# A hybrid encoder layer on one core: the split operands of each FFN phase moved to another byte offset in their buffers

## The chip, the core and the metric

The kernel runs on one core of a Trainium2 chip. The metric is the device time of one execution in microseconds, and lower is better. The program computes a whole encoder layer in float32 for 1024 rows of 1024 numbers.

## The reference, cut to what matters

```python
def swiglu_half_step(x, gain, w_in, w_out):          # w_in: 1024 x 5632, w_out: 2816 x 1024
    h = rms_norm(x, gain)
    gate, up = jnp.split(h @ w_in, 2, axis=-1)
    return (jax.nn.silu(gate) * up) @ w_out

x = x + 0.5 * swiglu_half_step(x, ffn1_norm, ffn1_w_in, ffn1_w_out)
x = x + hybrid_mixer(x, ...)      # attention heads and HGRN2 heads side by side, two projections
x = x + 0.5 * swiglu_half_step(x, ffn2_norm, ffn2_w_in, ffn2_w_out)
x = rms_norm(x, final_norm)
```

## The kernel before, in words

**Order of the work.** The program has four parts that follow each other: the first FFN (0 to about 750 us), the mixer's input projections with the recurrent heads (to about 1170 us), the attention with the output projections (to about 1410 us), and the second FFN. Each FFN has an up phase (`ffn_up`) and a down phase (`ffn_down`). A scheduler of the framework decides in which order each engine's instructions stand; within a pool, a tile waits until its buffer is free.

**Split operands.** Every large product is made of matmuls in the type float32r on TensorE. To keep float32 accuracy each operand is split into a high part and a low part (`split`, L98 to L103): ScalarE casts the source into the first half of a tile `hl` of shape [128, 2, 512] (L102), and VectorE writes source minus high part into the second half (L103). A product of two split operands is three matmuls: high by high, high by low, low by high. In a matmul one operand is stationary (loaded into the array by a weight load, PEld in the profile), and the other moves through it. In a row of the profile `py_ffn<-hl_out_ffn,hl_act_ffn` the result stands first, then the moving operand, then the stationary one.

**Up phase.** For 20 of the 22 blocks of 128 hidden units the up phase uses a Strassen-like scheme (`unit`, L293): seven products of 12 matmuls each, 84 matmuls of 128x128 by 128x512 per block, 1680 per FFN. The stationary operand is a split weight block, tile `hl_in_...` of the pool `wop`; the moving operand is a split activation block, tile `ffn_B` or `ffn_T` of the pools B and T, which lie at the high end of SBUF (`side="right"`) and stay for the whole phase. The first two blocks use plain products (`plain`, L276): 384 matmuls per FFN, 256 columns wide. Raw weights come by DMA into the pool `raw`, two tiles of 512 KB per block; the row tiles of x at the start of the phase use the same pool.

**Down phase.** For two groups g of four row tiles, and for the 22 blocks f, `operands` loads and splits the activations (`hl_act`, pool `ah`) and two halves of the weights (`hl_out_<ffn>_<f>_<g>_<d>`, pool `wo`), and `step` (L401) does 24 matmuls of 512 columns: 1056 per FFN. Here the stationary operand is `hl_act` and the moving one is `hl_out`. The last two blocks of a group (`tail`) are held back and done tile by tile.

**Where the buffers lie.** The start of a buffer in its partition, in the built program, as the remainder of its byte address by 64. Within a tile the matmuls' operands start at multiples of 512 bytes, so this remainder holds for every matmul.

| product | moving, before | stationary, before | moving, after | stationary, after |
|---|---|---|---|---|
| up, first FFN (L293, L276) | B, T: 32 | wop: 0 | 0 | 32 |
| up, second FFN | B, T: 32 | wop: 0 | 0 | 48 |
| down, first FFN (L401) | wo: 0 | ah: 0 | 0 | 16 |
| down, second FFN | wo: 0 | ah: 0 | 16 | 16 |
| mixer projections (L166, L494) | 32 | 32 | 0 | 0 |
| attention scores `s` (L797) | kT: 32 | qT: 0 | 0 | 0 |
| output projection `py` (L854) | hl_wor: 32 | recT: 0 | 0 | 0 |
| output projection `pa` (L854) | hl_woa: 32 | oT: 32 | 0 | 0 |
| attention values (L829) | pT: 32 | v_attn: 32 | 0 | 0 |

Before, the buffers of `wop`, `wo` and `ah` lie 4096 bytes apart; after, 4160 bytes (65 times 64).

The functions that the change touches, and what calls them:

Of the kernel before, what the change touches and what calls it, by code (L numbers as in the profile page):

```python
# [12 lines left out]
F32 = mybir.dt.float32  # L13
F32R = mybir.dt.float32r
# [7 lines left out]
P = 128  # L22
T = 1024
D = 1024
# [20 lines left out]
class Trunk:  # L45
    def __init__(self, ctx, tc, io):
        self.tc, self.nc, self.io = tc, tc.nc, io
        nc = self.nc
        pool = lambda name, **kw: ctx.enter_context(tc.tile_pool(name=name, **kw))
        self.const = pool("const", bufs=1)  # L50
        self.gpool = pool("gains", bufs=1)
        self.stat = pool("stat", bufs=4)
        self.dpool = pool("scratch", bufs=1, space=bass.MemoryType.DRAM)
        self.ident = self.const.tile([P, P], F32, name="ident")
        make_identity(nc, self.ident)
        self.banks = {}

# [111 lines left out]
                )  # L169


    def bank(self, name):
        return self.ps(name, "u")

# [12 lines left out]
    def ffn_up(self, name, pair, act, early_lo, mid):  # L187
# [53 lines left out]
            return [raw[j][:, k * 512 : (k + 1) * 512] for j in range(2) for k in range(2)]  # L241

        def weight_op(f, key, src, lo_engine=None):
            hl = self.wop.tile([P, 2, 512], F32R, name=f"hl_in_{name}_{f}_{key}", tag="wop")
            self.split(hl, src, lo_engine)
            return hl

# [51 lines left out]
        def unit(f):  # L299
# [8 lines left out]
            nc.scalar.copy(p1, a)  # L308
            yield
            b = bank("pb")  # L310
            product(b, A["A12"], "B21", True)
            g0 = result("g0", f)
# [34 lines left out]
        for f in range(early):  # L347
            A[f] = [weight_op(f, f"A{i}", src, early_lo) for i, src in enumerate(raw_weights(f))]
            plain(f, 0, A[f])
# [21 lines left out]
    def ffn_down(self, name, act, load, done, finish=None):  # L371

        nc = self.nc
        w_out = self.io[f"{name}_w_out"]
        tail = 2

        def operands(f, g):  # L380
            raw = self.draw.tile([P, 1024], F32, name=f"raw_out_{name}_{f}_{g}", tag="raw")
            nc.sync.dma_start(raw, w_out[f * P : (f + 1) * P, :])
            ar = self.ar.tile([P, 2, 256], F32, name=f"raw_act_{name}_{f}_{g}", tag="ar")
            nc.sync.dma_start(
                ar, act[f].rearrange("p (h t) -> p h t", h=2)[:, :, g * 256 : (g + 1) * 256]
            )
            ah = self.ah.tile([P, 2, 512], F32R, name=f"hl_act_{name}_{f}_{g}", tag="ah")
            self.split(ah, ar.rearrange("p h t -> p (h t)"))
            wo = []
            for d in range(2):  # L390
                hl = self.wo.tile([P, 2, 512], F32R, name=f"hl_out_{name}_{f}_{g}_{d}", tag="wo")
                self.split(hl, raw[:, d * 512 : (d + 1) * 512])
                wo.append(hl)
            return ah, wo

        def step(f, t, ops, py):
            ah, wo = ops
            o = (t % 2) * 256 + (t % 4) // 2 * P
            for d in range(2):
                for i, (a, b) in enumerate(((0, 0), (0, 1), (1, 0))):  # L400
                    nc.tensor.matmul(  # L401
                        py[d], ah[:, a, o : o + P], wo[d][:, b, :],
                        start=(f == 0 and i == 0), stop=(f == NF - 1 and i == 2),
                    )

        for g in range(2):
            tiles = range(4 * g, 4 * g + 4)
            py = {t: [self.bank(f"py_{name}_{t}_{d}") for d in range(2)] for t in tiles}
            x = {}
            late = []  # L410
            for f in range(NF):
                ops = operands(f, g)
                if f == 2:
                    for t in tiles:
                        x[t] = load(t)
                if f < NF - tail:
                    for t in tiles:
                        step(f, t, ops, py[t])
                else:
                    late.append((f, ops))  # L420
            for t in tiles:
                for f, ops in late:
                    step(f, t, ops, py[t])
                for d in range(2):
                    ds = slice(d * 512, (d + 1) * 512)
                    nc.vector.scalar_tensor_tensor(
                        out=x[t][:, ds], in0=py[t][d], scalar=0.5, in1=x[t][:, ds],
                        op0=ALU.mult, op1=ALU.add,
                    )
                done(t, x[t])  # L430
        if finish:
            finish()
# [535 lines left out]
def open_pools(ctx, tc, prefix, side="left", **spec):  # L968
    return {
        key: ctx.enter_context(  # L970
            tc.tile_pool(name=f"{prefix}_{key}", bufs=bufs, side=side, reuse_waits="tile")
        )
        for key, bufs in spec.items()
    }


def trunk_kernel(tc, io):
    nc = tc.nc
    with ExitStack() as ctx:
        k = Trunk(ctx, tc, io)  # L980
        rows = lambda a: [a[t * P : (t + 1) * P, :] for t in range(NT)]
        d = {key: rows(k.scratch(key, (T, D))) for key in ("x1", "x2", "x3", "xn2")}
# [9 lines left out]
        def ffn(ctx, name, xn_pair, load, done, d_spec, opened, early_lo, mid=None, finish=None):  # L992
            def sbuf(c, key, bufs, **kw):
                return c.enter_context(
                    tc.tile_pool(name=f"{name}_{key}", bufs=bufs, reuse_waits="tile", **kw)
                )

            k.open_psum(ctx, name, u=(8, 512))
            with ExitStack() as up:
                k.B, k.T = sbuf(up, "B", 4, side="right"), sbuf(up, "T", 3, side="right")  # L1000
                k.raw, k.wop, k.sums, k.snap, k.cc = (
                    sbuf(up, key, n)
                    for key, n in (("raw", 7), ("wop", 9), ("s", 4), ("n", 3), ("c", 4))
                )
                k.ffn_up(name, xn_pair, act, early_lo, mid)
            with ExitStack() as down:
                k.draw, k.ar, k.wo, k.ah = (
                    sbuf(down, key, n) for key, n in (("draw", 3), ("ar", 3), ("wo", 7), ("ah", 4))
                )
                pools = open_pools(down, tc, f"{name}_d", **d_spec)  # L1010
                opened(pools)
                k.ffn_down(name, act, lambda t: load(pools, t), lambda t, x: done(pools, t, x), finish)
# [3 lines left out]
        with ExitStack() as c1:  # L1016
            gain = []

            def pair1(i):
                x = []  # L1020
                for t in (2 * i, 2 * i + 1):
                    xt = k.raw.tile([P, D], F32, name=f"x_{t}", tag="raw")
                    nc.sync.dma_start(xt, x_in[t])
                    x.append(xt)
                if not gain:
                    gain.append(k.gain_row("ffn1_norm"))
                for xt, t in zip(x, (2 * i, 2 * i + 1)):
                    junk = k.wop.tile([P, D], F32R, name=f"junk_{t}", tag="wop").bitcast(F32)
                    k.norm_rows(xt, gain[0], xt, f"n0_{t}", junk=junk)
                return x  # L1030

            def load1(pools, t):
                xt = pools["x"].tile([P, D], F32, name=f"x0_{t}", tag="x")
                nc.sync.dma_start(xt, x_in[t])
                return xt

            gain_m = []

            def opened1(pools):
                k.hpool = hstack.enter_context(  # L1040
                    tc.tile_pool(name="hm", bufs=4, side="right", reuse_waits="tile")
                )
                hm.extend(k.new_h("hm"))
                k.wpool = hstack.enter_context(
                    tc.tile_pool(name="w2", bufs=3, side="right", reuse_waits="tile")
                )
                gain_m.append(k.gain_row("mix_norm"))

            def done1(pools, t, x):
                nc.sync.dma_start(d["x1"][t], x)  # L1050
                xns[t] = pools["xn"].tile([P, D], F32, name=f"xn_n1_{t}", tag="xn")
                k.norm_rows(x, gain_m[0], xns[t], f"n1_{t}", HALVES)
                if t >= 4:
                    k.rows_to_h(xns[t - 4], hm, t - 4, "n1", "u")

            def finish1():
                for t in range(4, NT):
                    k.rows_to_h(xns[t], hm, t, "n1", "u")

            ffn(c1, "ffn1", pair1, load1, done1, dict(x=4, xn=5), opened1, nc.gpsimd, lambda: k.vectors(k.raw), finish1)  # L1060

        with ExitStack() as c2:
# [92 lines left out]
```

## Time and profile before

| | us |
|---|---|
| median of 3 runs | 2145.54 |
| lowest and highest run | 2141.98, 2145.81 |
| the profiled execution, its own time | 2140.14 |
| its span, first to last instruction | 2138.4 |

All times in the profile are microseconds of this one profiled execution; means of one instruction are nanoseconds. PE is TensorE's matmuls, PEld its weight loads, DVE is VectorE, ACT is ScalarE, POOL is GpSimd, SP issues most DMAs. Matmuls are pipelined, and a matmul's shown duration reaches into the next ones. So the pace of the matmuls (start to start) is not the mean duration; it is read from a window in which nothing else runs on PE, or from a piece of the chain of waits, as length over count. In a window, a matmul counts if any of it lies inside, so the pace is (window + one duration) / count.

### The profile page before, as it was taken

How to read it: one execution, taken by the hardware profiler on the slowest of the kernel's cores; microseconds unless marked ns; L12 is line 12 of the kernel's file. 1: busy time of each engine (PE TensorE's matmuls, PEld its weight loads, DVE VectorE, ACT ScalarE, POOL GpSimd, SP SyncE). 2: the span in 40 equal slices, each digit the busy share in tenths (PEclk: the TensorE clock that was granted, in tenths of full speed). 3: DMA queues.
4: the chain of work that ended last, by engine and by line, in shares of the span. 5: the costliest groups of instructions: out<-in, count | busy, mean ns of one | idle time of the engine just before them, and what ended most of it. 6: DMA issues, size and time to landing. Idle time of an engine off the chain costs nothing.

```text
span 2138.4 us, 27958 instructions
## 1 busy us (share of the span) xinstructions
PE 2059.3 (96%) x10849; PEld 1754.6 (82%) x10849; DVE 1156.3 (54%) x1951; ACT 780.6 (37%) x1295; POOL 391.5 (18%) x278
## 2 busy tenths in 40 slices
PE   5899999999999999999999999988999999999998
PEld 5788878887888798989999788878888888878886
DVE  6555554535363515798872567754554554443634
ACT  4333343324343323333332546623333333333432
POOL 2333232210000000121120323313322222100000
PEclk9999999999999999999999999999999999999999
DMA  5422322127464211121234522353322221264542
GB/s 166 123 80 79 93 83 80 60 70 251 147 226 142 81 36 44 40 76 34 89 98 142 177 98 80 110 191 113 90 89 76 73 89 55 74 234 142 185 148 79
DMA packets 208124, 232.12 MB, mean 109 GB/s; under 512 B 9444, under 2 KB 169464, under 8 KB 207992
## 3 DMA queue, kind: packets, MB, share of 16 engines
q1 hardware_dynamic: 205688, 221.95, 32.9%
q0 software_dynamic: 2304, 8.39, 1.0%
q8 instruction: 85, 1.39, 0.3%
q14 instruction: 47, 0.39, 0.1%
HBM read 175.78 MB, written 54.53 MB: 108 GB/s over the span
## 4 chain that ended last, share of the span: by engine, by line
PE 91%; DVE 5%; DMA 2%; ACT 1%; issue 1%; POOL 0%; SPq 0%; DVEq 0%; ACTq 0%; POOLq 0%
PE py_ffn L401 22%; PE pa_ffn L293 16%; PE pd_ffn L293 10%; PE rec_ps L166 6%; PE pb_ffn L293 5%; PE pc_ffn L293 5%; PE pp_ffn L276 4%; PE ri_ps L494 2%; PE rg_ps L494 2%; PE py L854 2%; PE lv L560 2%; PE s L797 2%; PE pa L854 2%; PE pv L829 2%; PE aq_ps L494 1%; PE av_ps L494 1%
## 5 line engine op out<-in xcount | busy, mean ns | idle before, releaser
L401 PE MATMUL py_ffn<-hl_out_ffn,hl_act_ffn 128*128 128x512 f32 x2112 | 483.6, 391 | 3.5 <-ACT hl_out_ffn L102 3.4
L401 PEld LDWEIGHTS py_ffn<-hl_out_ffn,hl_act_ffn 128*128 128x128 f32 x2112 | 398.4, 189 | 87.8 <-ACT hl_out_ffn L102 5.0
L103 DVE TENSOR_TENSOR hl_out_ffn<-raw_out_ffn,hl_out_ffn 128x512 fp32r<-128x512 f32 x176 | 120.2, 689 | 235.7 <-ACT hl_out_ffn L102 235.5
L293 PE MATMUL pa_ffn<-ffn_T,hl_in_ffn_S 128*128 128x512 f32 x960 | 243.8, 396 | 0.0
L293 PEld LDWEIGHTS pa_ffn<-ffn_T,hl_in_ffn_S 128*128 128x128 f32 x960 | 180.9, 188 | 44.3
L102 ACT CAST hl_out_ffn<-raw_out_ffn 128x512 fp32r<-128x512 f32 x176 | 107.8, 620 | 266.8 <-PE py_ffn L401 251.2
L103 DVE TENSOR_TENSOR hl_in_ffn_S<-s_ffn,hl_in_ffn_S 128x512 fp32r<-128x512 f32 x160 | 162.6, 1019 | 30.5 <-ACT hl_in_ffn_S L102 30.5
L102 ACT CAST hl_in_ffn_S<-s_ffn 128x512 fp32r<-128x512 f32 x160 | 99.1, 621 | 204.6 <-PE pd_ffn L293 177.7
L103 DVE TENSOR_TENSOR hl_in_ffn_A<-raw_in_ffn,hl_in_ffn_A 128x512 fp32r<-128x512 f32 x128 | 101.0, 794 | 127.0 <-ACT hl_in_ffn_A L102 127.0
L102 ACT CAST hl_in_ffn_A<-raw_in_ffn 128x512 fp32r<-128x512 f32 x136 | 83.8, 624 | 182.5 <-PE pc_ffn L293 78.6
L166 PE MATMUL rec_ps<-hm,hl_rec_w 128*128 128x512 f32 x576 | 134.9, 392 | 0.0
L293 PE MATMUL pd_ffn<-ffn_T,hl_in_ffn_S 128*128 128x512 f32 x480 | 125.4, 396 | 0.0
L293 PE MATMUL pb_ffn<-ffn_B,hl_in_ffn_A 128*128 128x512 f32 x480 | 125.2, 397 | 0.0
L166 PEld LDWEIGHTS rec_ps<-hm,hl_rec_w 128*128 128x128 f32 x576 | 107.1, 188 | 21.8
L293 PE MATMUL pa_ffn<-ffn_B,hl_in_ffn_A 128*128 128x512 f32 x480 | 120.1, 399 | 0.0
L293 PE MATMUL pc_ffn<-ffn_T,hl_in_ffn_A 128*128 128x512 f32 x480 | 118.9, 396 | 0.0
L293 PE MATMUL pd_ffn<-ffn_B,hl_in_ffn_S 128*128 128x512 f32 x456 | 113.1, 397 | 0.0
L293 PEld LDWEIGHTS pa_ffn<-ffn_B,hl_in_ffn_A 128*128 128x128 f32 x480 | 90.9, 190 | 21.9
L293 PEld LDWEIGHTS pd_ffn<-ffn_T,hl_in_ffn_S 128*128 128x128 f32 x480 | 90.5, 188 | 22.1
L293 PEld LDWEIGHTS pc_ffn<-ffn_T,hl_in_ffn_A 128*128 128x128 f32 x480 | 90.4, 188 | 22.1
L293 PEld LDWEIGHTS pb_ffn<-ffn_B,hl_in_ffn_A 128*128 128x128 f32 x480 | 90.4, 188 | 21.9
L276 PE MATMUL pp_ffn<-ffn_B,hl_in_ffn_A 128*128 128x256 f32 x768 | 98.6, 289 | 7.3 <-ACT ffn_B L184 3.9
(245 smaller groups left out, 3128.8 us busy)
## 6 DMA issues: line engine op xcount, KB each, us to landing
raw_in_ffn<-in_ffn_w_in SPq DMA_DIRECT2D x88, 512.0 KB, 4.1
raw_out_ffn<-in_ffn_w_out SPq DMA_DIRECT2D x88, 512.0 KB, 3.7
raw_act_ffn<-d_act SPq DMA_DIRECT2D x88, 256.0 KB, 4.0
d_act<-g_ffn SPq DMA_DIRECT2D x80, 256.0 KB, 2.1
x<-d_x SPq DMA_DIRECT2D x24, 512.0 KB, 4.4
x<-in_x SPq DMA_DIRECT2D x16, 512.0 KB, 4.7
d_x<-x SPq DMA_DIRECT2D x16, 512.0 KB, 2.8
raw_rec_w<-in_w_in_mix SPq DMA_DIRECT2D x12, 512.0 KB, 3.8
```

Of the source, the lines that this page charges most:

```text
L102: nc.scalar.copy(hl[:, 0, :], src)
L103: (lo_engine or nc.vector).tensor_sub(hl[:, 1, :], src, hl[:, 0, :].bitcast(F32))
L166: nc.tensor.matmul(out, hl[:, a, ks], h[half][b][:, k, cols], start=(k == 0 and i == 0), stop=(k == NK - 1 and i == 2),)
L276: nc.tensor.matmul(ps[j][:, odd * 256 : (odd + 1) * 256], A[2 * j + k // 4][:, a, ks], B[k // 4][:, b, k % 4, cols], start=(k == 0 and i = ...
L293: nc.tensor.matmul(ps, A[:, a, ks], T[key][:, b, k, :], start=(first and k == 0 and i == 0), stop=(k == 3 and i == 2), skip_group_check=True,)
L401: nc.tensor.matmul(py[d], ah[:, a, o : o + P], wo[d][:, b, :], start=(f == 0 and i == 0), stop=(f == NF - 1 and i == 2),)
L494: nc.tensor.matmul(ps[:, tt, :], h[half][a][:, k, ts], hl[k // 4][:, b, ws], start=(k == 0 and i == 0), stop=(k == NK - 1 and i == 2),)
L560: nc.tensor.matmul(pl[:, cs], now[:, 0, cs], now[:, 1, cs], start=True, stop=True)
L797: nc.tensor.matmul(ps[:, ks], qT[:, a, qs], kT[:, b, kv, ks], start=(i == 0), stop=(i == 2))
L829: nc.tensor.matmul(ps, vt[:, j, a, vs], pT[j][:, b, i4, :], start=(st == 0 and i == 0), stop=(st == NT - 1 and i == 2),)
L854: nc.tensor.matmul(py, lhs(a, n), units[n][:, b, ds], start=(n == 0 and i == 0), stop=(n == 3 and i == 2),)
```

## The change

A tile of 32 bytes per partition is put at the high end of SBUF ahead of all others there, which moves every high-end buffer down by 32 bytes, to a multiple of 64. The tiles of `wop`, `ah` and `wo` become 1040 numbers long instead of 1024, and the split operand starts a few numbers into its tile: 8 numbers (32 bytes) for the first FFN's weight blocks, 12 (48 bytes) for the second's, 4 (16 bytes) for the activations of both down phases, 0 and 4 for the down weights of the first and the second FFN. The pool `raw` has 6 buffers instead of 7, and `wo` 6 instead of 7. No arithmetic is changed. Lines of the changed kernel stand up to 7 further down than those of the kernel before.

```diff
         self.ident = self.const.tile([P, P], F32, name="ident")
+        pool("align", bufs=1, side="right").tile([P, 8], F32, name="align")
...
+    def offset(self, pool, name, tag, o):
+
+        return pool.tile([P, 1040], F32R, name=name, tag=tag)[:, o : o + 1024].rearrange(
+            "p (a b) -> p a b", a=2
+        )
...
-            hl = self.wop.tile([P, 2, 512], F32R, name=f"hl_in_{name}_{f}_{key}", tag="wop")
+            hl = self.offset(self.wop, f"hl_in_{name}_{f}_{key}", "wop", 8 if name == "ffn1" else 12)
...
-            ah = self.ah.tile([P, 2, 512], F32R, name=f"hl_act_{name}_{f}_{g}", tag="ah")
+            ah = self.offset(self.ah, f"hl_act_{name}_{f}_{g}", "ah", 4)
...
-                hl = self.wo.tile([P, 2, 512], F32R, name=f"hl_out_{name}_{f}_{g}_{d}", tag="wo")
+                hl = self.offset(self.wo, f"hl_out_{name}_{f}_{g}_{d}", "wo", 0 if name == "ffn1" else 4)
...
-                    for key, n in (("raw", 7), ("wop", 9), ("s", 4), ("n", 3), ("c", 4))
+                    for key, n in (("raw", 6), ("wop", 9), ("s", 4), ("n", 3), ("c", 4))
...
-                    sbuf(down, key, n) for key, n in (("draw", 3), ("ar", 3), ("wo", 7), ("ah", 4))
+                    sbuf(down, key, n) for key, n in (("draw", 3), ("ar", 3), ("wo", 6), ("ah", 4))
...
-                    junk = k.wop.tile([P, D], F32R, name=f"junk_{t}", tag="wop").bitcast(F32)
+                    junk = k.wop.tile([P, 1040], F32R, name=f"junk_{t}", tag="wop").bitcast(F32)[:, 0:D]
```

The scheduler's order changes in a few places. On SP, at the start of the program, these are the first weight loads of the up phase before (`raw_in_ffn_<f>_<half>`, `x` the row tiles, `d_t_ffn` a store of a sum of row tiles, which waits for VectorE):

```order
L236 DMA raw_in_ffn_0_0_264<-in_ffn_w_in 128x8x128
L236 DMA raw_in_ffn_0_1_266<-in_ffn_w_in 128x8x128
L236 DMA raw_in_ffn_1_0_382<-in_ffn_w_in 128x8x128
L471 DMA g_attn_q_norm<-in_attn_q_norm 128x128
L471 DMA g_attn_k_norm<-in_attn_k_norm 128x128
L471 DMA g_rec_out_norm<-in_rec_out_norm 128x128
L223 DMA d_t_ffn_137<-t_ffn_0_500 128x512
L236 DMA raw_in_ffn_1_1_384<-in_ffn_w_in 128x8x128
L1023 DMA x_533<-in_x 128x1024
```

And the same place now:

```order
L243 DMA raw_in_ffn_0_0_268<-in_ffn_w_in 128x8x128
L243 DMA raw_in_ffn_0_1_270<-in_ffn_w_in 128x8x128
L478 DMA g_attn_q_norm<-in_attn_q_norm 128x128
L478 DMA g_attn_k_norm<-in_attn_k_norm 128x128
L478 DMA g_rec_out_norm<-in_rec_out_norm 128x128
L230 DMA d_t_ffn_141<-t_ffn_0_504 128x512
L243 DMA raw_in_ffn_1_0_386<-in_ffn_w_in 128x8x128
L243 DMA raw_in_ffn_1_1_388<-in_ffn_w_in 128x8x128
L1030 DMA x_537<-in_x 128x1024
```

The first weight tile of block 1 has moved behind the store of the first sum: it has no seventh buffer to go to.

On ACT, in the first FFN's down phase, at the change from the first group of row tiles to the second, these are the casts of the second group's weights for blocks 1 and 2 (`hl_out_ffn_<f>_<g>_<d>`), between the squares of the finished rows (`xn_n`), before:

```order
L102 CAST hl_out_ffn_1_1_0_4838<-raw_out_ffn_1_1_4831 128x512
L120 ACTIVATE xn_n_0_4673,ss_n_0_4674<-x_0_3971 128x512 x2
L120 ACTIVATE xn_n_1_4705,ss_n_1_4706<-x_1_3973 128x512 x2
L120 ACTIVATE xn_n_2_4737,ss_n_2_4738<-x_2_3975 128x512
L102 CAST hl_out_ffn_1_1_1_4841<-raw_out_ffn_1_1_4831 128x512
L120 ACTIVATE xn_n_2_4737,ss_n_2_4738<-x_2_3975 128x512
```

And now:

```order
L121 ACTIVATE xn_n_0_4677,ss_n_0_4678<-x_0_3975 128x512 x2
L121 ACTIVATE xn_n_1_4709,ss_n_1_4710<-x_1_3977 128x512 x2
L121 ACTIVATE xn_n_2_4741,ss_n_2_4742<-x_2_3979 128x512
L103 CAST hl_out_ffn_1_1_0_4842<-raw_out_ffn_1_1_4835 128x512
L121 ACTIVATE xn_n_2_4741,ss_n_2_4742<-x_2_3979 128x512
L103 CAST hl_out_ffn_1_1_1_4845<-raw_out_ffn_1_1_4835 128x512
```

Block 1's first weight half is cast where its second half was cast before, and the second half one square later. On PE the matmuls of the phases stand in the same order but for some twelve of them at this place and a few in the attention.

## The prediction

> **What bounds the kernel now.** I began with the page: engines, clock and the chain of work that ended last.
>
> ```profile
> span 2138.4 us, 27958 instructions
> PE 2059.3 (96%) x10849; PEld 1754.6 (82%) x10849; DVE 1156.3 (54%) x1951; ACT 780.6 (37%) x1295; POOL 391.5 (18%) x278
> ...
> PEclk9999999999999999999999999999999999999999
> ...
> PE 91%; DVE 5%; DMA 2%; ACT 1%; issue 1%; POOL 0%; SPq 0%; DVEq 0%; ACTq 0%; POOLq 0%
> ```
>
> TensorE is the bound: 91% of the chain, at a clock that is nearly always the full one. No other engine is busy for much over half the time. So what counts is the pace of the matmuls, start to start, and the second view is the windows of PE, over stretches in which only one product runs: up phase of the first FFN, its down phase, then the same two of the second FFN.
>
> ```profile
> 120.00:490.00 370.00, 370.00 (x1580) 1.00 0.25 78
> 500.00:600.00 100.00, 100.00 (x443) 1.00 0.63 204
> ...
> 1510.00:1880.00 370.00, 370.00 (x1581) 1.00 0.24 76
> 1900.00:2000.00 100.00, 100.00 (x443) 1.00 0.58 194
> ```
>
> The columns are the window, its length, PE's busy time with the matmuls in it, the clock, and DMA. The groups by line give the duration of one matmul:
>
> ```profile
> L401 PE MATMUL py_ffn<-hl_out_ffn,hl_act_ffn 128*128 128x512 f32 x2112 | 483.6, 391 | 3.5 <-ACT hl_out_ffn L102 3.4
> L293 PE MATMUL pa_ffn<-ffn_T,hl_in_ffn_S 128*128 128x512 f32 x960 | 243.8, 396 | 0.0
> ```
>
> Up: (370 + 0.396) / 1580 = 234.4 ns per matmul. Down: (100 + 0.391) / 443 = 226.6 ns. Both are 128x128 by 128x512 in the same type at full clock, with PE never idle, and both phases give the same in both FFNs. The difference of 7.8 ns needs a cause, and the table of buffer positions offers one: in the up phase the moving operand starts 32 bytes off the stationary one (by the remainder of 64), in the down phase both start alike. Four pieces of the chain of waits, each one product at a stretch, test this. Their columns are start, length and what.
>
> ```profile
> 30.46 22.53 PE pp_ffn L276 x192
> ...
> 798.59 38.11 PE rec_ps L166 x168
> ...
> 1120.96 46.09 PE rg_ps L494 x384
> ...
> 1205.61 5.15 PE py L854 x22
> ```
>
> `rec_ps` has both operands at 32, a distance of 0, and runs at 38.11 / 168 = 226.8 ns, the pace of the down phase, whose operands are both at 0. `py` in the attention has 32 against 0 and runs at 5.15 / 22 = 234.1 ns, the pace of the up phase. So the common position does not matter here, but the distance does: 0 gives 226.6, 32 gives 234.4. For 256 columns it looks different: `rg_ps` (distance 0) 46.09 / 384 = 120.0 ns, `pp` (distance 32) 22.53 / 192 = 117.3. At distance 0 the second 256 columns cost 226.8 - 120.0 = 106.8 ns, so 512 columns alone 213.6, and 13.2 ns lie beside the columns in each matmul. 213.6 is as low as a matmul of 512 columns can come by these rows.
>
> The trace holds only the distances 0 and 32. The change puts the up phase of the second FFN at 48 and the down phase of the first at 16. These two are the unknowns.
>
> **The change part by part**, against the profiled execution (span 2138.4, own time 2140.14 us). This is 5.4 us below the median of the three runs, 2145.54, so I add the sum to the median. A measurement of this kernel can tell about 0.2%, or 4.3 us, from no change.
>
> *First FFN, up, 1680 matmuls.* Before 0 against 32, now 32 against 0: the distance by 64 stays 32, and I take nothing. The ends: if it matters which operand is ahead, they go to 226.6 (1680 x -7.8 ns = -13.1 us), or lose as much again (+13.1).
>
> *Second FFN, up, 1680 matmuls.* From distance 32 to 48. By 64 bytes, 48 is 16 away from 0 and 16 away from 32, so neither row is nearer. I take the middle, 230.5 ns: 1680 x -3.9 = -6.6 us. The ends are the two rows: 0 and -13.1 us. Beyond them, the columns alone would be 1680 x -20.8 = -34.9 us, and as far above 234.4 as 0 is below it, +13.1.
>
> *First FFN, down, 1056 matmuls.* From distance 0 to 16, again in the middle of the two: 1056 x +3.9 = +4.1 us; ends 0 and +8.2 us, beyond them 1056 x -13.0 = -13.7 (columns alone) and +16.5.
>
> *Second FFN, down, 1056 matmuls.* Both at 16, distance 0. As 32 and 32 ran like 0 and 0, I take nothing; the end is +8.2 us, if a start that is no multiple of 32 costs as much as a distance.
>
> *Attention, 384 matmuls.* `s` and `py` go from distance 32 to 0. At -7.8 ns each that is -3.0 us. Not all of it arrives, since PE waits there for ACT and DVE at times:
>
> ```profile
> 1190.00:1440.00 250.00, 232.75 (x1396) 0.97 0.39 130
> ...
> L797 PE MATMUL s<-kT,qT 128*128 128x512 f32 x192 | 54.1, 418 | 6.8 <-ACT p L804 2.5 <-DVE qT L103 2.2 <-DVE kT L103 1.6
> ```
>
> PE is busy for 232.75 of 250 us. I take -2.0 us, ends -3.0 and 0.
>
> *Everything else on PE.* Mixer projections, `pa` and the attention values keep distance 0. The 256-column products of the second FFN move between 117.3 and 120.0 at most, 384 x 2.7 ns = 1.0 us; I take nothing.
>
> *Writing at offsets.* The splits on ACT and DVE now write at 16, 32 or 48. The trace has such writes at 32 (`pT`) beside those at 0 (`hl_out`):
>
> ```profile
> L103 DVE TENSOR_TENSOR hl_out_ffn<-raw_out_ffn,hl_out_ffn 128x512 fp32r<-128x512 f32 x176 | 120.2, 689 | 235.7 <-ACT hl_out_ffn L102 235.5
> L820 DVE TENSOR_TENSOR pT<-ptp,pT 128x512 fp32r<-128x512 f32 x64 | 43.0, 686 | 5.9 <-ACT pT L819 5.5
> ```
>
> 689 and 686 ns: nothing. And DVE mostly waits for ACT, which waits for PE, so a few per cent here would stay hidden.
>
> *One raw buffer less.* A load takes 4.1 us and a block of the up phase 84 x 0.2344 = 19.7 us; six tiles still hold three blocks. What now waits longer on SP's queue are the stores behind these loads, and nothing near reads them. At the start the first weight tile of block 1 stands behind a store that issued at 13.62 us:
>
> ```profile
> raw_in_ffn<-in_ffn_w_in SPq DMA_DIRECT2D x88, 512.0 KB, 4.1
> ```
>
> ```profile
> 13.62 0.36 SPq L223 DMA_DIRECT2D d_t_ffn<-t_ffn  x1
> ...
> 16.26 0.38 SPq L236 DMA_DIRECT2D raw_in_ffn<-in_ffn_w_in  x1
> ```
>
> Two loads are then issued where one was, at about 16 us, and land some 4 to 5 us later. Block 0's 192 matmuls begin only at 30.46, by the chain above. So this costs nothing, at most 1 us.
>
> *One `wo` buffer less.* At the change of groups the held-back blocks 20 and 21 keep four buffers and block 0 of the next group two, so block 1's weights are split later. The timelines of ACT and of DVE there, and the window of PE:
>
> ```profile
> 605.08 0.62 ACT L102 CAST hl_out_ffn<-raw_out_ffn 128x512 fp32r<-128x512 f32 x1
> ...
> 613.45 0.62 ACT L102 CAST hl_out_ffn<-raw_out_ffn 128x512 fp32r<-128x512 f32 x1
> ```
>
> ```profile
> 615.42 0.69 DVE L426 SCALAR_TENSOR_TENSOR x<-py_ffn,x 128x512 f32<-128x512 f32 x1
> ```
>
> ```profile
> 606.00:626.00 20.00, 20.00 (x90) 1.00 0.80 278
> ```
>
> By the order, block 1's first half moves from the row at 605.08 to about the one at 613.45, and its second half a cast or two behind it; with VectorE's subtraction (689 ns, after some of the norm's work) both are there by about 618. The held-back work is 4 x 12 matmuls, block 0 then runs for 24, so that block 1 is wanted some 18 matmuls (4.1 us) after the last of the held-back ones. These end at about 615, since DVE takes up their last tile at 615.42; so it is wanted near 619. PE was busy for all of these 20 us. I take nothing, and at most 1.5 us in each FFN.
>
> **The sum:** 0 - 6.6 + 4.1 + 0 - 2.0 + 0 = -4.5 us, thus 2145.5 - 4.5 = 2141.0 us. This case's own range is -9 to 0.
>
> [...]
>
> **The rivals.**
>
> *Cheap distances.* 48 runs as well as 0 (-13.1) and 16 costs nothing: with the attention -15.1 us, 2130.4; better than that if the 13.2 ns beside the columns shrink. For it: distance 0 is not free either, so some other distance may be better. Against it: the only other distance in the trace is worse.
>
> *Dear distances (slower).* Any distance but 0 sets the pace of 32: the second up phase stays (0), the first down phase goes to 234.4 (+8.2), attention -2.0: +6.2 us, 2151.7. The place is the window 500 to 600 us, and it decides from 5.9 ns per matmul on, where 1056 of them outweigh the attention and 4.3 us. For it: two rows cannot tell a smooth cost from a step.
>
> *The pitch (slower).* Buffers now lie 65 x 64 bytes apart instead of 4096. If the distance counts by 128 and not by 64, it changes from buffer to buffer: half of the second down phase gets 64 against 0 (528 x 7.8 = +4.1), the first down phase 16 or 80 (+8.2), attention -2.0: +10.3 us, 2155.8, and up to 25 if some distance is worse than 32. For it: every row before has the same distance by 128 within its kind, so none excludes it.
>
> *No effect.* The up phase differs from the down phase in something other than position, such as which operand stays for the phase. Then nothing moves, 2145.5 (at most 1 us either way). Against it: `py` and `rec_ps` have little in common with the phases whose pace they share. [...]
>
> **How the numbers follow.** Chances: the forecast 0.30, cheap distances 0.24, dear distances 0.20, the pitch 0.14, no effect 0.12. Faster by over 0.2%: all of cheap distances and 0.18 of the forecast, whose middle lies just beyond 4.3 us: 0.42. Within 0.2%: the rest of the forecast 0.12, no effect 0.12, and 0.01 of dear distances: 0.25. Slower: 0.19 + 0.14 = 0.33. The range goes from 2120 (cheap distances and a third of what lies down to the columns alone) to 2160 (the pitch with 4 us more). It leaves out about 0.1 below, where both new distances come near the columns alone, and 0.06 above.
>
> **What would show it.** In the changed profile, the same windows of PE: 120 to 490 us should hold 1580 matmuls (234.4 ns), 500 to 600 some 436 (230.5), the second FFN's up phase some 1607 in 370 us (230.5), and its down phase 443 in 100 us (226.6). `py` should take 22 x 0.2267 = 4.99 us, not 5.15. Between 606 and 626 us PE should have no idle time, and its first product of 256 columns should begin near 30.5 us. It is wrong if the first up phase or the second down phase changes its pace, since for these the rows of before say nothing should; if 16 or 48 runs above 234.4 or below 226.6; or if PE waits for weights.

## The result, and the profile after

The changed kernel takes 2151.12 us (median of 10 runs, 2147.00 to 2155.85), the kernel before 2144.52 us (10 runs on the same chip, 2139.16 to 2148.66). The ratio is 1.0033, 95% interval 1.0022 to 1.0045: slower by some 6.6 us, where 4.5 us less than before was forecast.

The first two lines of the page of the changed kernel:

```profile
span 2148.7 us, 27893 instructions
...
PE 2062.9 (96%) x10849; PEld 1753.0 (82%) x10849; DVE 1162.0 (54%) x1951; ACT 780.0 (36%) x1295; POOL 391.8 (18%) x278
```

TensorE is still the bound, with 90% of the chain of waits, so the question is again the pace of the matmuls and what holds up the starts of the phases. The windows of PE in the changed kernel (stretch, length, busy time and matmuls, clock, DMA):

```profile
120.00:490.00 370.00, 370.00 (x1586) 1.00 0.26 79
500.00:600.00 100.00, 100.00 (x431) 1.00 0.60 197
606.00:626.00 20.00, 20.00 (x88) 1.00 0.67 214
1190.00:1440.00 250.00, 231.52 (x1357) 0.97 0.38 127
1510.00:1880.00 370.00, 370.00 (x1603) 1.00 0.26 79
1900.00:2000.00 100.00, 100.00 (x434) 1.00 0.61 205
```

First FFN, up phase: (370 + 0.394) / 1586 = 233.5 ns, before 234.4. Second up phase: 370.394 / 1603 = 231.1. The two down phases: 100.395 / 431 = 232.9 and 100.395 / 434 = 231.3, before 226.6 in both. So the up phases got a little faster and both down phases much slower, the second one too, for which nothing was forecast. The chain of waits of the changed kernel has the products beside the FFNs and the end of the first FFN's start:

```profile
66.81 1.09 PE pt_ffn_T L188 x4
67.90 23.31 PE pp_ffn L283 x188
...
100.65 2.95 PE pa_ffn L300 x12
...
804.86 38.11 PE rec_ps L167 x168
...
1200.99 4.63 PE py L861 x20
```

`rec_ps` keeps its pace (226.8 ns); `py` goes to 4.63 / 20 = 231.5 ns, not to 226.7. And the last plain products of the first FFN begin at 67.90. In the chain of the kernel before, the same two pieces:

```profile
65.20 23.44 PE pp_ffn L276 x188
...
97.38 3.32 PE pa_ffn L293 x12
```

They began 2.7 us earlier, and so did the up phase behind them, by 3.3 us. The starts of the phases in the two traces show where the profiled 10.3 us went (2148.7 against 2138.4; the profiled run of before was 4.4 us under its median of ten, the one of after 0.6 us, so 3.8 us of it is scatter):

| stretch | longer by, us |
|---|---|
| start to first up-phase matmul | 3.3 |
| first up phase | -1.8 |
| first down phase and its norm | 6.0 |
| mixer | 0.0 |
| attention | 1.4 |
| start of the second FFN | 2.1 |
| second up phase | -4.5 |
| second down phase to the end | 4.0 |

The means from matmul to matmul over whole phases, taken from all starts in the trace (intervals over 280 ns left out), are used below as well: up 234.3 and 234.3 before, 233.4 and 231.1 after; down 226.7 and 226.7 before, 232.6 and 231.3 after.

### The profile page after: what moved, and what is told of

Same layout as the page of the kernel before. It is cut to its first block, busy times and chain, and to the rows that moved or that the text cites. A ratio compares the mean times of both kernels' runs of the same rounds, so it can differ in the third digit from the quotient of the medians.

```text
span 2148.7 us, 27893 instructions
## 1 busy us (share of the span) xinstructions
PE 2062.9 (96%) x10849; PEld 1753.0 (82%) x10849; DVE 1162.0 (54%) x1951; ACT 780.0 (36%) x1295; POOL 391.8 (18%) x278
## 4 chain that ended last, share of the span: by engine, by line
PE 90%; DVE 5%; DMA 2%; issue 1%; ACT 1%; POOL 0%; SPq 0%; DVEq 0%; ACTq 0%; POOLq 0%
PE py_ffn L408 22%; PE pa_ffn L300 16%; PE pd_ffn L300 10%; PE rec_ps L167 6%; PE pb_ffn L300 5%; PE pc_ffn L300 5%; PE pp_ffn L283 4%; PE rg_ps L501 2%; PE ri_ps L501 2%; PE py L861 2%; PE pa L861 2%; PE lv L567 2%; PE s L804 2%; PE pv L836 2%; PE aq_ps L501 1%
## 5 line engine op out<-in xcount | busy, mean ns | idle before, releaser
L408 PE MATMUL py_ffn<-hl_out_ffn,hl_act_ffn 128*128 128x512 f32 x2112 | 493.3, 395 | 4.3 <-ACT hl_out_ffn L103 3.4
```

Source lines behind the costliest of these rows:

```text
L408: nc.tensor.matmul(py[d], ah[:, a, o : o + P], wo[d][:, b, :], start=(f == 0 and i == 0), stop=(f == NF - 1 and i == 2),)
```

## The experiments

By the remainder of 64 bytes, on which the prediction rested, the first up phase and the second down phase should have stayed as they were. By the remainder of 256, the start of the stationary operand minus that of the moving one (the distance, from here on) was, in the built program, 96 in the up phases before, 0 in the down phases, in `rec_ps` and in `pa`, and 96 in `py` and `s`. In the changed kernel it is 128 in `py` and `s`, and in the FFNs it changes from buffer to buffer, since 4160 = 16 x 256 + 64. The theory was that the distance counts by 256; the rivals were that it counts by less, and that something else sets the pace.

**The buffers alone.** Raw and `wo` buffers cut, no operand moved:

```diff
-                    for key, n in (("raw", 7), ("wop", 9), ("s", 4), ("n", 3), ("c", 4))
+                    for key, n in (("raw", 6), ("wop", 9), ("s", 4), ("n", 3), ("c", 4))
...
-                    sbuf(down, key, n) for key, n in (("draw", 3), ("ar", 3), ("wo", 7), ("ah", 4))
+                    sbuf(down, key, n) for key, n in (("draw", 3), ("ar", 3), ("wo", 6), ("ah", 4))
```

> The kernel before with 6 buffers instead of 7 in raw and in wo, and nothing else; every buffer that TensorE reads keeps its distance of 0 or 96 bytes (by 256). Theory 'buffers cost at the start': the changed kernel lost 3.3 us before the first up phase and 2.1 us before the second, and those come from the raw pool; so about 5 us slower here (2147 to 2151 against 2144.5), the first up phase beginning near 100 us instead of 97.0, paces of 234.4 ns (up) and 226.6 ns (down) as before. Rival, as predicted at first: the buffers are free, 0 to 1 us, and the lost start belongs to the offsets or to chance.

Measured: 2147.26 against 2143.89 us, ratio 1.0018 (1.0010 to 1.0027), so about 3.9 us (2.1 to 5.8). The windows of PE of this kernel hold what before's held, but for one matmul:

```profile
500.00:600.00 100.00, 100.00 (x442) 1.00 0.63 203
1510.00:1880.00 370.00, 370.00 (x1581) 1.00 0.25 79
```

The paces are unmoved and the down phases, the only place of `wo`, are 0.0 and 0.2 us longer: the `wo` buffer costs nothing. What is left are the two FFN starts and the attention; in this profile the first start is 2.3 us longer. Two timelines show a cause for a part of it. In the kernel before, SP's next load after the row tiles is issued at 30.22, and ACT casts it at 35.53:

```profile
30.22 0.38 SPq L236 DMA_DIRECT2D raw_in_ffn<-in_ffn_w_in  x1
```

```profile
35.53 0.62 ACT L102 CAST hl_in_ffn_A<-raw_in_ffn 128x512 fp32r<-128x512 f32 x1 [0.49 <-DMA raw_in_ffn<-in_ffn_w_in]
```

With six buffers SP issues no weight load between 29.68 and 56.73, and ACT's cast stands at 60.64, amid the casts of `ffn_T` and `ffn_B` for which the transposes and the plain products wait:

```profile
29.68 0.87 SPq L1023 DMA_DIRECT2D x<-in_x  x2
...
56.73 1.77 SPq L236 DMA_DIRECT2D raw_in_ffn<-in_ffn_w_in  x2
```

```profile
58.09 1.34 ACT L184 CAST ffn_T<-pt_ffn_T 128x512 fp32r<-128x512 f32 x2
60.64 0.62 ACT L102 CAST hl_in_ffn_A<-raw_in_ffn 128x512 fp32r<-128x512 f32 x1 [1.22 <-DMA raw_in_ffn<-in_ffn_w_in]
```

ACT idles 1.22 us on the load and then casts for 0.62 us, and everything behind it on ACT waits for that long. In this kernel's chain the last plain products start at 67.62:

```profile
67.62 23.43 PE pp_ffn L276 x188
...
99.69 3.34 PE pa_ffn L293 x12
```

2.4 us after before's 65.20. Not all of that is the late load. By the starts in the two traces, the 192nd plain product is 1.3 us late already (53.99 us, 52.71 before), and that is ahead of the late load. From there to the 197th, the pause in which PE does transposes takes 13.29 us, 12.49 before. This pause is 12.5 us in all three kernels with seven raw buffers and 13.3 us in all seven with six, in both FFNs. So at the place of the late cast the missing buffer costs 0.8 us at each start, 1.6 of the 3.9 us in all; where the rest lies is not shown. Single profiles scatter too much for it: here the attention is 2.5 us longer and the start of the second FFN behind it 2.9 us, but the 48 matmuls of `pa` at the end of that attention take 12.63 us at a granted clock of 0.87, and 11.05 us at 1.00 before.

**The high end moved by 32 bytes.** The kernel before with only the first line of the change; up phases, `s` and `py` come to a distance of 128, which is 0 by 64:

```diff
+        pool("align", bufs=1, side="right").tile([P, 8], F32, name="align")
```

> The kernel before with only the 32-byte tile at the high end; no offsets, no fewer buffers. Up phases, scores and output projection py then have distance 0 by 64 but 128 by 256. Theory 'the distance counts by 256 bytes': up pace like that of py after the change, 232 to 233.5 ns in 120 to 490 us, thus 3 to 8 us faster than before. Rival 'by 64 bytes', the one of the prediction: up pace 226.6 ns, 26 to 28 us faster.

Measured: 2138.71 us, ratio 0.9977 (0.9967 to 0.9987). Its windows of PE:

```profile
500.00:600.00 100.00, 100.00 (x442) 1.00 0.63 203
1510.00:1880.00 370.00, 370.00 (x1594) 1.00 0.25 77
```

Up phase 370.394 / 1594 = 232.4 ns; the down phase stays at 227. A distance of 0 by 64 or by 128 does not give the pace of `rec_ps` (226.8). That one line, without the rest, would have been a gain of some 5 us.

**All starts at zero.** The changed kernel with the three offsets at 0; the tiles stay 4160 bytes apart:

```diff
-            hl = self.offset(self.wop, f"hl_in_{name}_{f}_{key}", "wop", 8 if name == "ffn1" else 12)
+            hl = self.offset(self.wop, f"hl_in_{name}_{f}_{key}", "wop", 0)
...
-            ah = self.offset(self.ah, f"hl_act_{name}_{f}_{g}", "ah", 4)
+            ah = self.offset(self.ah, f"hl_act_{name}_{f}_{g}", "ah", 0)
...
-                hl = self.offset(self.wo, f"hl_out_{name}_{f}_{g}_{d}", "wo", 0 if name == "ffn1" else 4)
+                hl = self.offset(self.wo, f"hl_out_{name}_{f}_{g}_{d}", "wo", 0)
```

> The changed kernel with all four offsets set to 0; tiles stay 4160 bytes apart and the pools as small. By 64 every distance is 0; by 256 it runs through 0, 64, 128 and 192 from buffer to buffer. Theory 'by 256': paces of 230 to 232 ns in all four phases, 2146 to 2151 us in all, no better than the changed kernel by more than 5 us. Rival 'by 64': 226.6 ns in all four phases, 2118 to 2124 us.

Measured: 2145.66 us, ratio 1.0010 (1.0001 to 1.0020). By 64 bytes every operand starts at the same place here, and yet:

```profile
500.00:600.00 100.00, 100.00 (x432) 1.00 0.60 192
...
1510.00:1880.00 370.00, 370.00 (x1601) 1.00 0.26 80
1900.00:2000.00 100.00, 100.00 (x432) 1.00 0.56 191
```

Up 231.4 ns, down 100.395 / 432 = 232.4 ns. The down phases lose 5.8 ns per matmul by the spacing of 4160 bytes alone, since the buffers and the high end by themselves did not move this pace (442 matmuls in 100 us, in both runs above). The count by 64 is excluded. The time and the down phases lie just outside what was expected by 256 (2146 to 2151 us, 230 to 232 ns).

**A spacing of 4352 bytes.** The changed kernel, its tiles 17 x 256 bytes apart, so that each phase has one distance: 160 and 176 in the up phases, 16 and 0 in the down phases; in the second of these both operands start at 16:

```diff
-        return pool.tile([P, 1040], F32R, name=name, tag=tag)[:, o : o + 1024].rearrange(
+        return pool.tile([P, 1088], F32R, name=name, tag=tag)[:, o : o + 1024].rearrange(
...
-                    junk = k.wop.tile([P, 1040], F32R, name=f"junk_{t}", tag="wop").bitcast(F32)[:, 0:D]
+                    junk = k.wop.tile([P, 1088], F32R, name=f"junk_{t}", tag="wop").bitcast(F32)[:, 0:D]
```

> The changed kernel, with its offsets, but with tiles of 4352 bytes (17 times 256), so that within each phase all buffers have one and the same distance by 256: 160 in the first up phase, 176 in the second, 16 in the first down phase, 0 in the second (both operands at 16 by 64). Theory 'by 256': second down phase back to 226.6 to 227 ns, first down phase 232 to 233.5, first up phase near 233.4, second near 230 (these by the matmuls of the changed kernel that have these distances). Rival 'the start at 16 bytes costs by itself': second down phase stays near 231.3 as in the changed kernel. Rival 'by 64': first up phase 234.4 and second down phase 226.6.

Measured: 2146.52 us, ratio 1.0013 (1.0002 to 1.0023).

```profile
120.00:490.00 370.00, 370.00 (x1586) 1.00 0.25 79
500.00:600.00 100.00, 100.00 (x430) 1.00 0.60 197
1510.00:1880.00 370.00, 370.00 (x1610) 1.00 0.25 79
1900.00:2000.00 100.00, 100.00 (x430) 1.00 0.58 196
```

160: 233.5 ns; 176: 230.1 ns; 16 in the down phase: 100.39 / 430 = 233.5. The last row is a miss of the theory: a distance of 0 should have given 226.7, and 233.5 came. Both operands at 16 is not the same as both at 0, or both at 32 as in `rec_ps` before. In this phase all but 4 of the 1055 intervals from start to start are 233 or 234 ns: every matmul pays alike, so it is not a few of them waiting for their operands.

**The high end moved by 160 bytes.** The kernel before with one line, which puts every matmul of 512 columns in the FFNs and the attention at a distance of 0. It takes 160 bytes of each partition, and no buffer had to go for it:

```diff
+        pool("align", bufs=1, side="right").tile([P, 40], F32, name="align")
```

> The kernel before with a tile of 160 bytes instead of none at the high end, and nothing else. All moving and stationary operands of the up phases, the scores and py then have distance 0 by 256 and start at multiples of 64; buffers stay at 7 and 4096 bytes apart. Theory 'distance by 256': up pace 226.7 ns, 3360 times 7.6 ns less, 22 to 29 us faster (2115 to 2122). Rival 'what the phases multiply sets the pace, not where it lies': 234.3 ns and no change.

Measured: 2116.39 us (5 runs, 2112.99 to 2124.16) against 2144.26, ratio 0.9879 (0.9858 to 0.9900). It beats both kernels. The page and the windows of PE:

```profile
span 2114.8 us, 27958 instructions
...
PE 2033.2 (96%) x10849; PEld 1753.3 (83%) x10849; DVE 1166.7 (55%) x1951; ACT 780.7 (37%) x1295; POOL 392.1 (19%) x278
```

```profile
120.00:220.00 100.00, 100.00 (x443) 1.00 0.26 81
...
500.00:600.00 100.00, 100.00 (x443) 1.00 0.57 184
...
1510.00:1610.00 100.00, 100.00 (x443) 1.00 0.27 82
```

Up and down phases now hold the same 443 matmuls in 100 us, 226.6 ns each. In the chain of this kernel `py` has it as well, 4.53 / 20 = 226.5 ns:

```profile
1181.25 4.53 PE py L855 x20
```

The two up phases are 13.1 and 12.4 us shorter than before; 1680 x 7.7 = 12.9 us each. So it is the distance, not which operand stays or what the phase does, that made the up phase slower than the down phase: going from a distance of 96 to 0 is worth 1.2% of the kernel. How a distance comes to cost time is not shown; the runs show only that it does.

**A map of distances.** Three kernels, tiles 4352 bytes apart, high end moved by 160 bytes, six buffers of `raw` and of `wo`, run once each. The edit is the spacing above with the starts as offsets in bytes:

| kernel | wop, first FFN | wop, second | ah, first | ah, second | wo, first | wo, second |
|---|---|---|---|---|---|---|
| first | 64 | 192 | 32 | 224 | 0 | 0 |
| second | 256 | 16 | 0 | 32 | 16 | 32 |
| third | 32 | 240 | 128 | 16 | 0 | 0 |

```diff
+            hl = self.offset(self.wop, f"hl_in_{name}_{f}_{key}", "wop", 16 if name == "ffn1" else 48)
...
+            ah = self.offset(self.ah, f"hl_act_{name}_{f}_{g}", "ah", 8 if name == "ffn1" else 56)
...
+                hl = self.offset(self.wo, f"hl_out_{name}_{f}_{g}_{d}", "wo", 0)
```

(This is the first kernel's; the numbers in the code are floats of 4 bytes.)

> The changed kernel with tiles 4352 bytes apart, the high end moved by 160 bytes so that offsets are distances by 256, and other offsets: stationary 64 ahead in the first up phase, 192 in the second, 32 in the first down phase, 224 in the second; moving at 0. All starts are multiples of 32. Theory 'distance by 256', from the matmuls that had these distances in passing: 229 to 233 ns for 64, 229 to 231 for 192, 233 for 32 and 224; each phase with one pace of its own, none at 226.7. Rival 'only starts off a multiple of 32 cost, and distances that change from buffer to buffer': all four phases at 226.7.

> As the run with 64 and 192, with these offsets: stationary 256 ahead in the first up phase, 16 in the second; in the first down phase the moving operand at 16 and the stationary at 0; in the second both at 32. Theory 'distance by 256, and starts at a multiple of 32': 226.7 ns at 256 and at both 32; 233 ns at 16 in the up phase as in the down phase with tiles of 4352 bytes, and near 233 with the moving operand at 16. Rival 'the distance counts by 512 or more': 256 costs like the others, 229 to 234. Rival 'any start but 0 costs': both at 32 near 233 as both at 16.

> Buffers a multiple of 256 bytes apart, high end moved down by 160 bytes. The starts: stationary operand 32 bytes ahead of the moving one in the first up phase, 16 behind (240) in the second, 128 ahead in the first down phase, 16 ahead in the second; every moving operand starts at the same place by 256. Theory A: the distance by 256 bytes alone sets the pace, in both phases alike. It then gives 233.3 ns at 32 (as the down phase measured), 232.4 at 128 (as the up phase measured), and one value at 16 that must be both 226.67 (up phase) and 233.34 (down phase), so A already has a row against it there; it survives only if the down phase at 16 comes out at 226.7 this time. Theory B: the phase counts too, up and down each having a table of its own by distance; then the second down phase gives 233.3 again at 16, and 32 and 128 need not agree with the other phase. Theory C: some distance is better than 0; then 240 gives under 226.6. If 240 only mirrors 224 and 192, it gives 227 to 233.

Measured: 2144.69, 2121.32 and 2134.61 us, one run each. The windows of PE of the first, the second and the third:

```profile
120.00:490.00 370.00, 370.00 (x1587) 1.00 0.25 79
500.00:600.00 100.00, 100.00 (x430) 1.00 0.60 199
...
1510.00:1880.00 370.00, 370.00 (x1618) 1.00 0.26 81
1900.00:2000.00 100.00, 100.00 (x430) 1.00 0.55 186
```

```profile
120.00:220.00 100.00, 100.00 (x443) 1.00 0.27 82
...
500.00:600.00 100.00, 100.00 (x433) 1.00 0.54 183
...
1510.00:1610.00 100.00, 100.00 (x442) 1.00 0.29 87
...
1900.00:2000.00 100.00, 100.00 (x443) 1.00 0.48 153
```

```profile
120.00:220.00 100.00, 100.00 (x431) 1.00 0.26 79
...
500.00:600.00 100.00, 100.00 (x432) 1.00 0.60 202
...
1510.00:1610.00 100.00, 100.00 (x443) 1.00 0.26 79
...
1900.00:2000.00 100.00, 100.00 (x430) 1.00 0.47 156
```

All that the runs with one distance per phase gave for matmuls of 512 columns, as means from matmul to matmul:

| distance | up phase, ns | down phase, ns |
|---|---|---|
| 0 | 226.7 | 226.7; both at 32: 226.7; both at 16: 233.3 |
| 16 | 226.7 | 233.3 |
| 32 | 233.3 | 233.3 |
| 64 | 233.3 | |
| 96 | 234.3 | |
| 128 | 232.4 | 232.4 |
| 160 | 233.3 | |
| 176 | 230.0 | |
| 192 | 228.9 | |
| 224 | | 233.3 |
| 240 | 226.7 | 231.7 (moving operand at 16) |

256 bytes ahead runs as 0 does (the second kernel, first up phase: 443 in 100 us, 226.6 ns) and 128 does not (232.4), so in these runs the distance repeats at 256. At 32 (233.3) and at 128 (232.4), up and down agree. Near 0 they do not: 16 either way is free in the up phase (226.7 ns) and costs 5 to 6.6 ns in the down phase (231.7 and 233.3). The expectation of the distance alone fails there, and its rival, that the phase counts too, holds. Why was not found. In the up phases the two operands lie in far regions of SBUF and in the down phases close by, but a kernel with the two exchanged was not tried. No distance gave less than 226.7. The rows do not simply add up where the distance changes from buffer to buffer: with all starts at zero the up phases pass through 0, 64, 128 and 192, whose rows have the mean 230.3, and 231.4 came.

All this holds for 512 columns. The plain products of 256 columns follow another order. These are windows of PE in which they run alone, in the kernel with 160 bytes (distance 0) and in the first kernel of the map (distance 64):

```profile
36.00:50.00 14.00, 14.00 (x119) 1.00 0.17 56
```

```profile
36.00:50.00 14.00, 14.00 (x126) 1.00 0.15 56
```

That is 120.0 ns at a distance of 0 and 113.3 at 64, where 512 columns are dear. And 256 does not settle their pace: at the same distance of 96 they ran at 117.3 ns in the first FFN of before and at 118.7 in its second and in both of the kernel with fewer buffers. Why is open.

## Why the prediction was wrong

- **The step that failed first** is the table of positions by the remainder of 64: "the distance by 64 stays 32, and I take nothing". What repeats is 256 (226.6 ns there, 232.4 at 128). The two rows of before had the distances 0 and 96 by 256, which by 64 look like 0 and 32; they show that a distance costs (226.6 and 234.4), and could not show its modulus. The first up phase, taken at 0, gained 1.8 us; its tiles pass through 32, 96, 160 and 224, whose rows in the table (224 from a down phase) have the mean 233.6 ns, and 233.4 came.
- **Second up phase, -6.6 us:** -4.5 measured. The pace is 231.1, the middle taken was 230.5. Nearly right in size, for no good reason: the 48 by 64 is four distances in turn.
- **First down phase, +4.1 us:** +6.0. The middle was 230.5 and 232.6 came. With offsets at zero it is 232.1, so most of it is the spacing, not the 16.
- **Second down phase, 0:** +4.0. "As 32 and 32 ran like 0 and 0, I take nothing" holds for 32 (the second map kernel, 443 in 100 us) and fails for 16, which alone costs 6.6 ns (the spacing of 4352); and the spacing of 4160 moves the distance in any case. The end named there, +8.2 if a start that is no multiple of 32 costs, is near what both at 16 cost in that run, 1056 x 6.6 = 7.0 us; in the change itself the two causes are not told apart.
- **Attention, -2.0:** `py` went to a distance of 128 by 256 and from 234.2 to 232.6 ns in the mean of all its matmuls (231.5 in the piece of the chain), `s` from 233.4 to 232.3. 384 x -1.4 = -0.5 us. The stretch as a whole is 1.4 us longer; in the profiles of the other kernels the same stretch is 2.1 us shorter to 7.3 us longer than before, so this is not put down to the change.
- **One raw buffer, 0, at most 1:** about 3.9 us in the run by itself (the profile of the change itself is 5.4 us longer at the two FFN starts). The runs place 0.8 us of it at the late cast of each start; where the rest lies is open. The prediction followed the load at 16 us, which is hidden, and not the seventh load. That was the one at 30.22, and what it delayed was not TensorE's need for those weights but ACT, which idled 1.22 us on the load, cast for 0.62 us, and only then went on with the casts of `ffn_B` and `ffn_T`.
- **"213.6 is as low as a matmul of 512 columns can come":** this floor, on which the lower ends of the range rest, came from 226.8 less 120.0 at a distance of 0. With 113.3 ns for 256 columns at a distance of 64 the same subtraction gives no fixed 13.2 ns beside the columns, so the floor is not shown. Nor is 117.3 ns the price of a distance for 256 columns, since 118.7 stands at the same one.
- **The `wo` buffer, and writing at offsets, 0:** right. PE is busy for all of 606 to 626, and VectorE's split of `hl_out` takes 691 ns (689 before).

The sum by the measured steps: buffers 3.9; the FFN phases by their means, 1680 x (-0.9 - 3.2) + 1056 x (5.9 + 4.6) = -6.9 + 11.1 = 4.2; attention -0.5: 7.6 us, against 6.6 (4.7 to 9.7 by the interval) measured.

Of the rivals, the pitch came nearest in kind (2155.8): the spacing does change the distance from buffer to buffer, and the down phases pay, the second too. Its modulus of 128 was wrong, and it had no gain in the up phases. Dear distances gave the total to 0.6 us (2151.7), but that was luck, by a sum that did not happen: the second up phase did gain and the second down phase did lose. No effect is ruled out, by the run with 160 bytes.

## What to carry to other kernels

Compare the starts of a matmul's two operands by the remainder of 256 bytes, for every buffer of a pool and not for the first alone. For matmuls of 512 columns equal remainders, at multiples of 32, gave the best pace in every phase here (226.7 ns, up to 234.3 at other distances), and one padding tile bought it; for 256 columns a distance of 0 was slower (120.0 ns) than one of 64 (113.3), so each size has to be measured. A tile whose length is no multiple of 256 bytes gives the buffers of a pool different distances. Before a buffer is given up, find the load that takes its place, and then look at who stands in order behind the instruction that waits for that load, on every engine.

## What the runs showed of the hardware that was not expected

- The pace of a 512-column matmul of this type, with as many weight loads as matmuls (10849 each on the page), goes from 226.7 to 234.3 ns with the distance of its operands, at the full clock and with PE never idle; a distance of 128 gives 232.4, so the cost does not simply grow as the two starts lie further apart.
- The pace of 256 columns goes another way: 120.0 ns at a distance of 0, 113.3 at 64, both at the full clock. The gain of the 160 bytes was had in spite of it.
- Both operands starting at 16 by 64 bytes cost 6.6 ns per matmul in the down phase (233.3 against 226.7), both at 32 nothing (226.7). Why is not shown.
- The same distance of 16 is free in the up phase (226.7) and dear in the down phase (233.3). This is left open.
